# An mLSTM and window-attention layer: a convolution behind the first head's key scaling, and the first FFN weight casts behind the heads' last cast

## The chip, the cores and the metric

The kernel runs on one core of one Trainium2 chip. The time is the device time of one execution in microseconds. Before the change three runs took 1243.84, 1246.0 and 1246.75 us, median 1246.0. The execution that was profiled took 1243.28 us.

## The reference

One encoder layer on 1024 tokens of width 1024, in float32. One input projection feeds two groups of heads. Group A are four mLSTM heads of width 128, in both directions; group B are windowed attention heads. Their outputs are concatenated, projected, added to `alpha*x` and normalised; a gated feed-forward block with a second normalisation follows. The change touches group A and the way into the feed-forward block:

```python
qk = silu(centred_dwconv(x @ Wqk, conv_w, conv_b))      # 5 taps along the tokens, per channel
q, k = split(qk)                                         # 4 heads x 128 each
# per direction, per chunk of 64 tokens:
s   = einsum('td,sd->ts', qc, kc) * w_intra
num = s @ vc + w_inter * (C applied to qc)
h   = num / max(|den|, exp(-m))
C   = decay * C + einsum('s,se,sd->ed', wa, vc, kc)      # keys scaled by wa
# directions summed, normalised per head over its 128 channels, times norm_g * sigmoid(o)
x   = LN(alpha * x + concat(h, attention) @ Wout)
x   = LN(alpha * x + (silu(x @ Wg) * (x @ Wu)) @ Wo + sigmoid(x @ Wpg) * (p @ Wp))
```

## The kernel before

Every matmul is done as three (`mm3`, L126 to L129): each operand is split into a high and a low part (`split`, L106 to L113: ScalarE casts the high part, VectorE or GpSimd subtracts it for the low part), and high x high, high x low and low x high are summed in PSUM. TensorE (PE) is therefore the engine with the most work.

The stages follow each other: input projections and attention to about 226 us; the four mLSTM heads to about 434 us, with the remaining projections as fillers between a head's steps; the second half of the output projection and the first normalisation to about 500 us; the feed-forward block, the gate and its output projection to 1209 us; the second normalisation to the end.

What sets the order. The kernel is written with a scheduling framework: within a stage it decides, from its own cost table and due times, in which order each engine's instructions are put; an engine then runs its instructions strictly in that order. Two things bind the scheduler. While `strict[0]` is true (L333 to L551, and from L860 to L995), TensorE keeps the order of the program. And `tc.issue_after(ins)` puts what is issued inside it behind `ins` on the same engine; it is an order, not a semaphore. The heads' stage is left to the scheduler, so one new bound can move many instructions behind it.

A tile of the query and key projection is `qk_tile(ct)` (L287): tiles 0 and 1 are head 0's q and k, tile 2 is head 1's q, and so on. Each tile is made in two halves of 512 tokens in one of three PSUM banks `pj`; ScalarE copies a half into `pre` (L294; there is one buffer of that name), and VectorE then runs the convolution over 1024 tokens: one tensor_scalar (L297) and four scalar_tensor_tensor (L299). A Silu on ScalarE follows.

A head (`mlstm_head`, L571) does, for each half of its tokens: transposes of k into a PSUM bank `kp`; the key scaling `ks`, by ScalarE for the forward direction (L590) and by VectorE for the backward one (L593); later `pp` = q times k. `kp`, `pp` and `tr` (the transposes of the finished head) share two PSUM banks, so a `pp` can begin only when both scalings have read the `kp` that was in its bank. Then come the weights `mw` (a DMA, two GpSimd operations L624 and L631, exponentials on ScalarE, L628 on VectorE), the state updates `up` and `C`, four chunks of `nd`, their division and statistics, and one `rs` on GpSimd (L660), after which VectorE scales `hs` (L662) and TensorE transposes it.

At the end of the heads, `finish` (L678) splits the gated output `so` into `mh` (ScalarE) and `ml` (VectorE). `out_proj` (L688) multiplies it into `yo` and adds it to `y` (L699 for the half of the attention heads, L701 for the half of the mLSTM heads). Its banks are the three `pj` too. `wino_w1` (L837) loads the first weights of the feed-forward block, `rg`, and casts them: `a1h` on ScalarE, `a1l` on GpSimd.

Of the kernel before, what the change touches and what calls it, by code (L numbers as in the profile page):

```python
# [10 lines left out]
ALU = mybir.AluOpType  # L11
# [4 lines left out]
P = 128  # L16
D = 1024
S = 1024
# [17 lines left out]
def hybrid_layer(  # L36
# [7 lines left out]
    act, dve, pool = nc.scalar, nc.vector, nc.gpsimd  # L44
# [43 lines left out]
    def W(shape, dt, name, bufs=1, tag=None):  # L88
        return cur["wk"].tile(shape, dt, name=name, tag=tag or name, bufs=bufs)

    def X(shape, dt, name):
        return xp.tile(shape, dt, name=name, tag="X", bufs=NX)

    def Y(shape, dt, name):
        return yp.tile(shape, dt, name=name, tag="Y", bufs=8)

    def bank(name, tag):
        return cur["ps"].tile([P, 512], F32, name=name, tag=tag, bufs=cur["psn"][tag])

    def pjb(name):  # L100
        return pj.tile([P, 512], F32, name=name, tag="pj")

    def flat(t):
        return t.rearrange("p a b -> p (a b)")

    def split(dst_hi, dst_lo, src, eng_lo=None):  # L106
        act.copy(dst_hi, src)  # L107
        if eng_lo == "halves":
            for c in range(2):
                cs = slice(c * 512, c * 512 + 512)  # L110
                pool.tensor_tensor(dst_lo[:, cs], src[:, cs], dst_hi[:, cs].bitcast(F32), ALU.subtract)
            return
        (eng_lo or pool).tensor_tensor(dst_lo, src, dst_hi.bitcast(F32), ALU.subtract)  # L113

    def load_w(src, shape, name, eng_lo=None, raw=None):
# [4 lines left out]
        lo = wp.tile([P] + shape, F32R, name="lo_" + name, tag="wlo", bufs=4)  # L120
        split(flat(hi), flat(lo), flat(raw), eng_lo or "halves")
        return hi, lo

    last = {}

    def mm3(o, ah, al, bh, bl, start, stop, goes_on=False):  # L126
        pe.matmul(o, ah, bh, start=start, stop=False, skip_group_check=goes_on)
# [12 lines left out]
    def fill(n):  # L140
        while n:
            if not running:
                if not fillers:
                    return
                f = fillers.pop(0)
                f["load"]()
                for g in fillers[:1]:
                    g["load"]()
                running.append(f["body"]())
            with tc.high_priority(offset=-100):  # L150
                got = next(running[0], None)
            if got is None:
                running.pop()
            else:
                n -= 1
# [3 lines left out]
    def fillr():  # L159
        owed[0] += RM  # L160
        fill(int(owed[0]))
        owed[0] -= int(owed[0])

    def drain(n=0):
        while len(fillers) + len(running) > n:
            fill(1)
# [10 lines left out]
    def proj_T(src, name, evac):  # L177
        def body(w):
            wh, wl = w
            for hf in range(2):  # L180
                o = pjb("pj_" + name)
                for kt in range(KT):
                    kp, j = divmod(kt, 2)
                    mm3(o, wh[:, kt, :], wl[:, kt, :], xh[kp, hf][:, j, :], xl[kp, hf][:, j, :], kt == 0, kt == KT - 1)
                    yield 1
                evac(o, hf)
            done.add(name)

        return filler(lambda: load_w(src, [8, P], name), body)
# [69 lines left out]
    colt = const.tile([P, 8, 8], F32, name="colt")  # L259
# [27 lines left out]
    def qk_tile(ct):  # L287
        def evac(o, hf):
            if hf == 0:
                pre = qk["pre", ct] = prep.tile([P, S + 4], F32, name="pre", tag="pre")  # L290
                dve.memset(pre[:, 0:2], 0.0)
                dve.memset(pre[:, S + 2:S + 4], 0.0)
            pre = qk["pre", ct]
            act.copy(pre[:, 2 + hf * 512:514 + hf * 512], o)  # L294
            if hf == 1:
                y = qk[ct] = Y([P, S], F32, f"qk{ct}")
                dve.tensor_scalar(y, pre[:, 0:S], colt[:, ct, 0:1], colt[:, ct, 5:6], ALU.mult, ALU.add)  # L297
                for w in range(1, 5):
                    dve.scalar_tensor_tensor(y, pre[:, w:w + S], colt[:, ct, w:w + 1], y, ALU.mult, ALU.add)  # L299
                act.activation(y, y, AF.Silu)  # L300

        return proj_T(wqk[ct], f"qk{ct}", evac)
# [67 lines left out]
    cA, cWA, cFL, cDE = (gcol[:, i, :] for i in range(4))  # L370
# [186 lines left out]
    mh, ml = {}, {}  # L557
# [13 lines left out]
    def mlstm_head(h):  # L571
# [7 lines left out]
        ks = {}  # L579
        for hf in range(2):  # L580
            kp_ = bank("kp", "ma")
            for cc in range(4):
                c = hf * 4 + cc
                pe.transpose(kp_[:, cc * P:(cc + 1) * P], kT[:, c * P:(c + 1) * P], ident)
            for d in range(2):
                kk = W([P, 4, P], F32, f"ks{d}{hf}", 4, "ks")
                if d == 0:
                    for cc in range(4):
                        r = col(d, hf * 4 + cc)
                        act.activation(kk[:, cc, :], kp_[:, cc * P:(cc + 1) * P], AF.Copy, scale=cWA[:, r:r + 1])  # L590
                else:
                    r = col(d, hf * 4)
                    dve.tensor_tensor(kk, kp_.rearrange("p (c k) -> p c k", k=P),  # L593
                                      cWA[:, r:r + 4].unsqueeze(2).to_broadcast([P, 4, P]), ALU.mult)
                ks[d, hf] = kk
            fillr()
        orders = (list(range(8)), list(range(7, -1, -1)))
        for g in range(3):
            for d in range(2):
# [3 lines left out]
                for i, idx in enumerate(idxs):  # L603
                    c = order[idx]
                    last["up", g] = pe.matmul(up[:, i * 129:i * 129 + 129], ks[d, c // 4][:, c % 4, :], va_[:, c, :], start=True, stop=True)
                for i, idx in enumerate(idxs):
                    c, nx = order[idx], order[idx + 1]
# [6 lines left out]
        for hf in range(2):  # L614
# [5 lines left out]
            for d in range(2):  # L620
                mw = W([P, 4, 2, P], F32, f"mw{h}{hf}{d}", 4, "mw")
                nc.sync.dma_start(mw, mwd[d, h, hf * 4:hf * 4 + 4].rearrange("c q t -> (c q t)").unsqueeze(0).to_broadcast([P, 1024]))
                w = mw[:, :, 0, :]
                pool.tensor_tensor(w, mw[:, :, 0, :], maskb[:, d, :].unsqueeze(1).to_broadcast([P, 4, P]), ALU.add)  # L624
                for cc in range(4):
                    r = col(d, hf * 4 + cc)
# [10 lines left out]
            for cc in range(4):  # L637
                c = hf * 4 + cc
# [39 lines left out]
    def finish(h, hf):  # L678
        hp, hj = divmod(h, 2)
        if hj == 0:  # L680
            mh[hp, hf] = X([P, 2, 512], F32R, f"mh{hp}{hf}")
            ml[hp, hf] = X([P, 2, 512], F32R, f"ml{hp}{hf}")
        split(mh[hp, hf][:, hj, :], ml[hp, hf][:, hj, :], sod[h][:, hf * 512:hf * 512 + 512], dve)
# [4 lines left out]
    def out_proj(t, nh, kps, u, first):  # L688
        hf, tt = divmod(t, 4)
        s = slice(tt * P, (tt + 1) * P)  # L690
        o = pjb("yo")
        for kp in kps:
            for j in range(2):
                mm3(o, mh[kp, hf][:, j, s], ml[kp, hf][:, j, s], u[nh, kp][0][:, j, :], u[nh, kp][1][:, j, :],
                    kp == kps[0] and j == 0, kp == kps[1] and j == 1)
                yield 1
        ys = ya[t][:, nh * 512:nh * 512 + 512]
        if first:
            dve.scalar_tensor_tensor(ys, ys, ALPHA, o, ALU.mult, ALU.add)  # L699
        else:  # L700
            dve.tensor_tensor(ys, ys, o, ALU.add)  # L701
            if nh == 0:
                stat[t] = W([P, 2, 6], F32, "st1", 8)
            dve.bn_stats(stat[t][:, nh, :], ys)
# [20 lines left out]
    for h in range(MH):  # L725
        mlstm_head(h)
        if h:
            gated(h - 1, last["up", 0])
# [4 lines left out]
    gated(MH - 1, last["mm"])  # L733
    for hf in range(2):
        finish(MH - 1, hf)
    drain()

    scope_s.close()
# [61 lines left out]
    def ln1_tr(t, late=False):  # L800
        tt = t % 4
        if t == 0:
            bx["b11"], bx["b21"] = new_block((F4, F4), "b11"), new_block((F4, F4), "b21")
        if t == 4:
            bx["b22"] = new_block((F4, F4), "b22")
        if t < 4:
            tr_block((t, t + 1), 0, bx["b11"], tt, b_lo)
            tr_block((t, t + 1), 512, bx["b21"], tt, b_hi)
        else:
            tr_block((t, t + 1), 512, bx["b22"], tt, b_hi, late)  # L810
# [26 lines left out]
    def wino_w1(i, new):  # L837
        rg, ru = new(f"rg{i}"), new(f"ru{i}")
        nc.sync.dma_start(rg, wffi[i, 0])
        nc.sync.dma_start(ru, wffi[i, 1])  # L840
        if i < 2:
            p1 = [X([P, 8, P], F32R, f"a1{c}{i}") for c in "hl"]
        else:
            p1 = w_pair(i, 1)
        split(flat(p1[0]), flat(p1[1]), flat(rg), "halves" if i < 2 else dve)
        return rg, ru, p1

    def w_pair(i, k):
        return (wp.tile([P, 8, P], F32R, name=f"a{k}h{i}", tag="whi", bufs=4),
                wp.tile([P, 8, P], F32R, name=f"a{k}l{i}", tag="wlo", bufs=4))  # L850
# [10 lines left out]
    for t in range(NT):  # L861
        for nh in range(2):
            list(out_proj(t, nh, (0, 1), u, False))
            if (t, nh) in TR1:
                ln1_tr(TR1[t, nh])
            if (t, nh) == (7, 0):
                t_sums(0, (pool, dve))
            if (t, nh) == (3, 1):
                ws = [wino_w1(0, raw8), wino_w1(1, raw8f)]
        ln1_norm(t)  # L870


# [201 lines left out]
    for i in range(FT):  # L1074
# [6 lines left out]
        w = w2[i] if i < 2 else wino_w2(i, *ws[i])  # L1081
# [275 lines left out]
```

## Time and profile before

| | us |
|---|---|
| median of three runs | 1246.0 |
| the profiled execution | 1243.28 |
| its span in the trace | 1241.4 |
| TensorE busy within the span | 1206.1 |
| VectorE busy | 843.4 |
| ScalarE busy | 511.2 |
| GpSimd busy | 404.7 |

The span runs from the first to the last instruction in the trace; 1.9 us of the execution lie outside it. "Idle" of an engine is time without an instruction on it. A line such as `tr L60 <- DVE hs L662` says that TensorE's transposes at L60 waited for the tile `hs` that VectorE wrote at L662. PE is TensorE, DVE is VectorE, ACT is ScalarE, POOL is GpSimd and SP is SyncE, whose queue issues the DMAs.

### The profile page before, as it was taken

The page shows a single profiled execution, that of the slowest core. Times are in us where ns is not written, and L with a number is a line of the kernel's source. Part 1 is how long each engine was busy: PE and PEld are TensorE (multiplying, and loading weights), DVE is VectorE, ACT ScalarE, POOL GpSimd, SP SyncE. Part 2 cuts the span into 40 slices and gives each one's busy share as a digit, 9 for nine tenths or more (in the row PEclk, how much of TensorE's full clock was granted, in tenths as well). Part 3 has the DMA queues.
Part 4 walks back from the last instruction along what each step waited for, and adds up shares of the span by engine and source line. Part 5 has one row for each costly group of instructions (what it writes and reads, how often), then busy time and mean ns, then how long its engine had stood idle before and what let it go on. Part 6 is the DMA issues. An engine that isn't in the chain of part 4 may idle for free.

```text
span 1241.4 us, 16496 instructions
## 1 busy us (share of the span) xinstructions
PE 1206.1 (97%) x6017; PEld 1006.0 (81%) x6017; DVE 843.4 (68%) x1546; ACT 511.2 (41%) x920; POOL 404.7 (33%) x321
## 2 busy tenths in 40 slices
PE   8999999999989999899999999999999999999996
PEld 8888888788778877688888888888887888888885
DVE  6865545868778778856667577576568696555566
ACT  5655443544563234623334233343343333333331
POOL 4543322616334025612322223323227440000017
PEclk9999999999999999899999999999999999999998
DMA  6321112313174142134545453465335556666503
GB/s 232 102 88 69 44 60 93 116 34 120 51 261 151 59 140 85 35 128 130 217 165 193 165 206 135 162 218 188 128 118 209 208 187 219 192 197 189 186 1 135
DMA packets 68784, 174.39 MB, mean 140 GB/s; under 512 B 7328, under 2 KB 12128, under 8 KB 68704
## 3 DMA queue, kind: packets, MB, share of 16 engines
q1 hardware_dynamic: 68704, 173.35, 41.1%
q8 instruction: 47, 0.77, 0.3%
q14 instruction: 33, 0.27, 0.1%
HBM read 126.86 MB, written 46.47 MB: 140 GB/s over the span
## 4 chain that ended last, share of the span: by engine, by line
PE 79%; DVE 9%; DMA 3%; POOL 2%; issue 2%; ACT 2%; POOLq 0%; SPq 0%; ACTq 0%; DVEq 0%
PE ma L56 19%; PE mc L56 9%; PE oa L56 7%; PE ob L56 7%; PE yo L56 5%; PE pj_qk L56 5%; PE mb L56 4%; PE pg L56 4%; PE pn_v L56 3%; PE pj_aq L56 2%; PE pj_o L56 2%; PE op L56 2%; PE sp L56 1%; PE nd L56 1%; PE et L60 1%
## 5 line engine op out<-in xcount | busy, mean ns | idle before, releaser
L944 POOL TENSOR_TENSOR s<-ru,rg 128x512 f32<-128x512 f32 x22 | 30.0, 1364 | 179.7 <-DMA ru<-in_wffi_dram 163.3
L1273 POOL TENSOR_TENSOR rs<-rs,mhalf 128x1 f32<-128x1 f32 x8 | 9.4, 1184 | 183.0 <-DVE rs L1272 182.9
L499 POOL TENSOR_SCALAR e<-e,st 128x384 f32<-128x384 f32 (+1 forms) x64 | 35.0, 561 | 93.8 <-DVE st L497 54.7
L1015 DVE TENSOR_TENSOR us<-us,ma 128x512 f32<-128x512 f32 x22 | 15.1, 685 | 66.7 <-PE ma L56 66.7
L56 PE MATMUL yo<-hi_wo,mh 128*128 128x512 f32 x128 | 51.5, 403 | 2.6 <-DVE y L701 2.0
L299 DVE SCALAR_TENSOR_TENSOR qk<-pre,colt,qk 128x1024 f32<-128x1024 f32 x32 | 51.7, 1615 | 0.6
L56 PE MATMUL pj_qk<-xh,hi_qk 128*128 128x512 f32 x128 | 51.5, 402 | 0.0
L56 PE MATMUL pj_qk<-xl,hi_qk 128*128 128x512 f32 x128 | 50.7, 396 | 0.0
L56 PE MATMUL pj_qk<-xh,lo_qk 128*128 128x512 f32 x128 | 50.6, 396 | 0.0
L56 PE MATMUL yo<-lo_wo,mh 128*128 128x512 f32 x128 | 50.2, 392 | 0.0
L953 POOL TENSOR_TENSOR s<-ru 128x512 f32<-128x512 f32 x22 | 37.0, 1681 | 40.6 <-DVE a2l L113 36.9
L56 PE MATMUL yo<-hi_wo,ml 128*128 128x512 f32 x128 | 49.8, 392 | 0.0
L107 ACT CAST a2h<-s 128x512 fp32r<-128x512 f32 x44 | 25.9, 619 | 54.0 <-PE mc L56 39.5
L107 ACT CAST a4h<-s 128x512 fp32r<-128x512 f32 x22 | 13.7, 621 | 83.6 <-PE ma L56 49.1
L949 POOL TENSOR_TENSOR s<-rg,s 128x512 f32<-128x512 f32 x22 | 28.7, 1303 | 53.9 <-DVE a4l L113 53.9
L489 DVE CUSTOM_DVE_ANT_0 e<-sp,bias 128x384 f32<-128x384 f32 (+1 forms) x64 | 31.2, 521 | 19.7 <-PE sp L56 17.8
L495 ACT ACTIVATE e<-e,st 128x384 f32<-128x384 f32 (+1 forms) x64 | 37.2, 583 | 8.4 <-DVE st L491 8.4
L1010 DVE TENSOR_TENSOR yb<-yb,us 128x512 f32<-128x512 f32 x22 | 37.1, 1684 | 0.3 <-ACT yb L1009 0.3
L511 ACT COPY eT<-et 128x384 f32<-128x384 f32 (+1 forms) x32 | 14.4, 450 | 54.6 <-PE et L60 54.4
L921 DVE TENSOR_TENSOR sa<-sb,sa 128x512 f32<-128x512 f32 x11 | 8.1, 732 | 41.1 <-DMA sb<-in_wffo_dram 41.1
L56 PE MATMUL mb<-b21h,a1h 128*128 128x512 f32 x88 | 35.1, 399 | 0.7 <-DVE ya L1015 0.7
L624 POOL TENSOR_TENSOR mw<-mw,maskb 128x512 f32<-128x512 f32 x16 | 23.6, 1476 | 37.1 <-PE pj_o L56 17.7
(905 smaller groups left out, 4205.2 us busy)
## 6 DMA issues: line engine op xcount, KB each, us to landing
fb<-hb SPq DMA_DIRECT2D x35, 512.0 KB, 4.4
rg<-in_wffi_dram SPq DMA_DIRECT2D x22, 512.0 KB, 3.5
ru<-in_wffi_dram SPq DMA_DIRECT2D x22, 512.0 KB, 5.1
fa<-sb SPq DMA_DIRECT2D x20, 512.0 KB, 3.5
mw<-mwd SPq DMA_DIRECT2D x16, 512.0 KB, 5.3
fa<-in_wffo_dram SPq DMA_DIRECT2D x15, 512.0 KB, 3.8
hb<-ya SPq DMA_DIRECT2D x11, 512.0 KB, 3.8
hb<-yc SPq DMA_DIRECT2D x11, 512.0 KB, 2.9
```

Of the source, the lines that this page charges most:

```text
L56: return pe.put(nc.tensor.matmul(*args, **kw))
L107: act.copy(dst_hi, src)
L299: dve.scalar_tensor_tensor(y, pre[:, w:w + S], colt[:, ct, w:w + 1], y, ALU.mult, ALU.add)
L489: dve.tensor_tensor_reduce(e[:, i, :L], sp[:, :L], biasd[j][:, i, off:off + L], 1.0, -BIG, ALU.add, ALU.max, accum_out=st[:, i:i + 1])
L495: act.activation(e[:, i, :L], e[:, i, :L], AF.Exp, bias=st[:, i:i + 1], accum_out=st[:, 2 + i:3 + i])
L499: pool.tensor_scalar(e[:, i, :L], e[:, i, :L], st[:, 6 + i:7 + i], 0.0, ALU.mult, ALU.add)
L624: pool.tensor_tensor(w, mw[:, :, 0, :], maskb[:, d, :].unsqueeze(1).to_broadcast([P, 4, P]), ALU.add)
L944: pool.tensor_tensor(s3, ru[:, lo, :], rg[:, lo, :], ALU.subtract)
L949: pool.tensor_tensor(s4, rg[:, up, :], s2, ALU.subtract)
L953: pool.tensor_tensor(s1, ru[:, lo, :], ru[:, up, :], ALU.add)
L1010: dve.tensor_tensor(hb_, hb_, u, ALU.mult)
L1015: (eng or dve).tensor_tensor(dst, x, y_, ALU.add)
```

## The change

The convolution of tile 2 (head 1's q) is put behind `last["ks"]` on VectorE, the key scaling of head 0's second half. And the casts of the first two feed-forward weight tiles (`wino_w1(0)`, `wino_w1(1)`) are put behind `last["mh"]` on ScalarE, the last cast of the heads' output. Nothing is added to or taken out of the computation; one activation table load less is issued on ScalarE (857 instructions for 858). The counts of the other engines stay.

```diff
     def split(dst_hi, dst_lo, src, eng_lo=None):
-        act.copy(dst_hi, src)
+        last["hi"] = act.copy(dst_hi, src)
...
                 y = qk[ct] = Y([P, S], F32, f"qk{ct}")
-                dve.tensor_scalar(y, pre[:, 0:S], colt[:, ct, 0:1], colt[:, ct, 5:6], ALU.mult, ALU.add)
-                for w in range(1, 5):
-                    dve.scalar_tensor_tensor(y, pre[:, w:w + S], colt[:, ct, w:w + 1], y, ALU.mult, ALU.add)
+                with tc.issue_after(last["ks"].ins) if ct == 2 else ExitStack():
+                    dve.tensor_scalar(y, pre[:, 0:S], colt[:, ct, 0:1], colt[:, ct, 5:6], ALU.mult, ALU.add)
+                    for w in range(1, 5):
+                        dve.scalar_tensor_tensor(y, pre[:, w:w + S], colt[:, ct, w:w + 1], y, ALU.mult, ALU.add)
...
-                    dve.tensor_tensor(kk, kp_.rearrange("p (c k) -> p c k", k=P),
+                    last["ks"] = dve.tensor_tensor(kk, kp_.rearrange("p (c k) -> p c k", k=P),
...
         finish(MH - 1, hf)
+    last["mh"] = last["hi"]
...
             if (t, nh) == (3, 1):
-                ws = [wino_w1(0, raw8), wino_w1(1, raw8f)]
+                with tc.issue_after(last["mh"].ins):
+                    ws = [wino_w1(0, raw8), wino_w1(1, raw8f)]
```

The lines of the changed kernel are one to three higher than those of the kernel before. No engine's order changes ahead of about 232 us, and none changes from the first whole feed-forward block on (about 510 us). In between the scheduler's order changes on all of them.

VectorE at the end of head 0's key transposes; `qk_2483` is tile 2, `ks_2384` and `ks_2402` are head 0's two backward key scalings. Before:

```order
L297 TENSOR_SCALAR qk_2483<-pre,colt 128x1024
L299 SCALAR_TENSOR_TENSOR qk_2483<-pre,colt,qk_2483 128x1024 x2
L593 TENSOR_TENSOR ks_2384<-kp,gcol 128x512
L299 SCALAR_TENSOR_TENSOR qk_2483<-pre,colt,qk_2483 128x1024
L593 TENSOR_TENSOR ks_2402<-kp,gcol 128x512
```

and now:

```order
L594 TENSOR_TENSOR ks_2384<-kp,gcol 128x512
L594 TENSOR_TENSOR ks_2402<-kp,gcol 128x512
L298 TENSOR_SCALAR qk_2483<-pre,colt 128x1024
L300 SCALAR_TENSOR_TENSOR qk_2483<-pre,colt,qk_2483 128x1024
L610 COPY C_2372<-up 128x129
L300 SCALAR_TENSOR_TENSOR qk_2483<-pre,colt,qk_2483 128x1024
```

Both scalings now stand ahead of the convolution, and the first state copy and four `mw` operations have come between its pieces. TensorE waits for the scalings with `pp`; at the same place its rows read, before:

```order
L56 MATMUL up<-va,ks_2379 128x129 x3
L56 MATMUL pj_qk_2593<-xh_120,lo_qk_2361 128x512
L56 MATMUL pj_qk_2593<-xh_132,hi_qk_2360 128x512
L56 MATMUL pj_qk_2593<-xl_133,hi_qk_2360 128x512
L56 MATMUL pj_qk_2593<-xh_132,lo_qk_2361 128x512
L56 MATMUL pj_qk_2593<-xh_132,hi_qk_2360 128x512
L56 MATMUL pp<-qk_2225,qk_2344 128x128 x8
```

and now:

```order
L56 MATMUL up<-va,ks_2379 128x129 x3
L56 MATMUL pj_qk_2593<-xh_120,lo_qk_2361 128x512
L56 MATMUL pp<-qk_2225,qk_2344 128x128 x4
L56 MATMUL pj_qk_2593<-xh_132,hi_qk_2360 128x512
L56 MATMUL pj_qk_2593<-xl_133,hi_qk_2360 128x512
L56 MATMUL pp<-qk_2225,qk_2344 128x128 x4
```

The two `pp` of head 0 have come forward by four and two projection matmuls.

GpSimd at the second half of the third head (its weight tiles are `mw_3467` and `mw_3476`, forward and backward; the `rs` between belongs to the head before). Before:

```order
L624 TENSOR_TENSOR mw_3467<-mw_3467,maskb 128x4x128
L631 TENSOR_TENSOR mw_3467<-qk_2854,mw_3467 128x4x128
L660 TENSOR_TENSOR rs<-rs,mhalf 128x4
L624 TENSOR_TENSOR mw_3476<-mw_3476,maskb 128x4x128
L631 TENSOR_TENSOR mw_3476<-qk_2854,mw_3476 128x4x128
L113 TENSOR_TENSOR lo_wo_3765<-raw_wo_3762,hi_wo_3764 128x1024
```

and now:

```order
L625 TENSOR_TENSOR mw_3467<-mw_3467,maskb 128x4x128
L632 TENSOR_TENSOR mw_3467<-qk_2854,mw_3467 128x4x128
L625 TENSOR_TENSOR mw_3476<-mw_3476,maskb 128x4x128
L632 TENSOR_TENSOR mw_3476<-qk_2854,mw_3476 128x4x128
L661 TENSOR_TENSOR rs<-rs,mhalf 128x4
L115 TENSOR_TENSOR lo_wo_3771<-raw_wo_3768,hi_wo_3770 128x1024
```

The `rs` has moved behind two operations; a low part of an output weight still stands behind it, the next one of the four.

ScalarE at the end of the heads; `mh_4107` is the heads' last cast, `a1h_4558` the first feed-forward weight. Before:

```order
L653 ACTIVATE hs<-nd,den 128x128 x3
L107 CAST hi_wo_4343<-raw_wo_4341 128x1024
L107 CAST hi_wo_4349<-raw_wo_4347 128x1024
L107 CAST a1h_4558<-rg_4554 128x1024
L107 CAST mh_4107<-so_3844 128x512
```

and now:

```order
L654 ACTIVATE hs<-nd,den 128x128 x3
L109 CAST hi_wo_4343<-raw_wo_4341 128x1024
L109 CAST hi_wo_4349<-raw_wo_4347 128x1024
L109 CAST mh_4107<-so_3844 128x512
L109 CAST a1h_4558<-rg_4554 128x1024
```

The two casts have changed places.

## Rows read from the trace of the kernel before

**Rows 1.** The page, part 1: busy time, share of the span, instructions.

```profile
PE 1206.1 (97%) x6017; PEld 1006.0 (81%) x6017; DVE 843.4 (68%) x1546; ACT 511.2 (41%) x920; POOL 404.7 (33%) x321
```

**Rows 2.** The windows view: stretch, PE, PEld, DVE, ACT, POOL busy, PEclk, DMA share, GB/s.

```profile
527.00:930.00 403.00, 403.00 (x1780) 333.93 (x1779) 259.78 (x343) 143.08 (x231) 117.97 (x81) 1.00 0.47 165
```

**Rows 3.** Waits of PE, 205 to 600 us: us in total, times, longest.

```profile
PE tr L60 <- DVE hs L662: 3.9, 3, 1.8
...
PE pp L56 <- DVE ks L593: 2.2, 2, 1.2
PE yo L56 <- DVE y L701: 2.0, 2, 1.5
...
PE nd L56 <- DVE hs L654: 1.0, 1, 1.0
...
PE up L56 <- DVE C L611: 0.7, 1, 0.7
```

**Rows 4.** Timeline of PE: start us, us, instruction, [idle before <-releaser].

```profile
226.20 1.03 PE L60 MATMUL kp<-ident,qk 128*128 128x128 f32 x8
...
234.60 1.16 PE L56 MATMUL pp<-qk,qk 128*128 128x128 f32 x8 [1.21 <-DVE ks L593]
```

**Rows 5.** Timeline of DVE, same place.

```profile
228.37 1.11 DVE L297 TENSOR_SCALAR qk<-pre,colt 128x1024 f32<-128x1024 f32 x1 [5.48 <-ACT pre L294]
...
233.87 0.68 DVE L593 TENSOR_TENSOR ks<-kp,gcol 128x512 f32<-128x512 f32 x1
...
236.67 1.27 DVE L299 SCALAR_TENSOR_TENSOR qk<-pre,colt,qk 128x1024 f32<-128x1024 f32 x1
```

**Rows 6.** Timeline of ACT, same place.

```profile
231.59 1.12 ACT L590 ACTIVATE ks<-kp,gcol 128x128 f32<-128x128 f32 x4
...
238.94 0.56 ACT L294 COPY pre<-pj_qk 128x512 f32<-128x512 f32 x1
```

**Rows 7.** The windows view, behind the wait at 316 us; columns as Rows 2.

```profile
316.00:320.00 4.00, 3.62 (x11) 2.99 (x12) 4.00 (x8) 1.14 (x4) 0.24 (x1) 0.57 0.47 131
```

**Rows 8.** Timeline of PE, the wait at 360 us.

```profile
359.87 0.33 PE L60 MATMUL tr<-ident,hs 128*128 128x128 f32 x1 [1.53 <-DVE hs L662]
```

**Rows 9.** Timeline of DVE: three half heads' scalings of hs.

```profile
313.10 3.23 DVE L662 TENSOR_SCALAR hs<-hs,mv,rs 128x128 f32<-128x128 f32 x4 [1.14 <-POOL rs L660]
...
354.94 5.13 DVE L662 TENSOR_SCALAR hs<-hs,mv,rs 128x128 f32<-128x128 f32 x4 [0.16 <-POOL rs L660]
...
429.09 1.12 DVE L662 TENSOR_SCALAR hs<-hs,mv,rs 128x128 f32<-128x128 f32 x4
```

**Rows 10.** Timeline of POOL beside the second of them.

```profile
353.88 1.02 POOL L660 TENSOR_TENSOR rs<-rs,mhalf 128x4 f32<-128x4 f32 x1
...
356.12 1.29 POOL L631 TENSOR_TENSOR mw<-qk,mw 128x512 f32<-128x512 f32 x1
357.37 2.36 POOL L113 TENSOR_TENSOR lo_wo<-raw_wo,hi_wo 128x1024 fp32r<-128x1024 f32 x1
```

**Rows 11.** The chain that ended last, 436 to 442 us.

```profile
436.43 0.62 ACT mh L107
...
437.07 1.37 DVE ml L113
...
438.46 3.45 DMA y<-in_xn_dram
```

**Rows 12.** Timeline of all engines at the output projection's second half.

```profile
434.31 0.74 DVE L675 SCALAR_TENSOR_TENSOR so<-tr,colt,so 128x512 f32<-128x512 f32 x1
...
435.47 1.05 ACT L107 CAST a1h<-rg 128x1024 fp32r<-128x1024 f32 x1 [3.39 <-DMA rg<-in_wffi_dram]
...
438.36 0.67 DVE L701 TENSOR_TENSOR y<-y,yo 128x512 f32<-128x512 f32 x1
...
439.08 0.50 PE L56 MATMUL yo<-hi_wo,mh 128*128 128x512 f32 x1 [1.54 <-DVE y L701]
...
442.68 0.50 PE L56 MATMUL yo<-hi_wo,mh 128*128 128x512 f32 x1 [0.57 <-DVE y L699]
```

More of the change, by code (lines that the diff above doesn't have):

```diff
@@ L101, in pjb @@
         return pj.tile([P, 512], F32, name=name, tag="pj")
+    last = {}
     def flat(t):
@@ L122, in load_w @@
         return hi, lo
-    last = {}
     def mm3(o, ah, al, bh, bl, start, stop, goes_on=False):
@@ L592, in mlstm_head @@
                     r = col(d, hf * 4)
-                    dve.tensor_tensor(kk, kp_.rearrange("p (c k) -> p c k", k=P),
-                                      cWA[:, r:r + 4].unsqueeze(2).to_broadcast([P, 4, P]), ALU.mult)
+                    last["ks"] = dve.tensor_tensor(kk, kp_.rearrange("p (c k) -> p c k", k=P),
+                                                   cWA[:, r:r + 4].unsqueeze(2).to_broadcast([P, 4, P]), ALU.mult)
                 ks[d, hf] = kk
```

## The prediction

> **What bounds the kernel now.** The page's first part comes first: TensorE is busy for 1206.1 of 1241.4 us [rows 1], so only its idle time can be won, some 35 us. The windows view then says where none is: from 527 to 930 us TensorE is busy in all 403 of 403 us [rows 2]. What is won before that stage is thus not given back in it, and its order is not touched; a gain in the heads is a gain at the end. The list of TensorE's waits from 205 to 600 us names what there is to win around the change [rows 3]: transposes for the scaled head `hs` (3.9 us in three waits), the scores `pp` for the key scaling (2.2 in two), the output projection for `y` (2.0 in two), `nd` (1.0) and `up` (0.7). The two edits aim at the second and the third. The scheduler moves the places of the others too, so each gets a term.
>
> **The scores.** The keys are transposed at 226.20 in 1.03 us, and the first `pp` starts at 234.60 after 1.21 us of waiting [rows 4]. On VectorE the convolution of tile 2 begins at 228.37, after 5.48 idle us, and the first scaling runs only at 233.87 (0.68 us); the last piece ends at 236.67 + 1.27 = 237.94 [rows 5]. With the scalings ahead, both fit where VectorE was idle: from about 227.3 to 227.3 + 2 x 0.68 = 228.7, while ScalarE needs until 231.59 + 1.12 = 232.71 for its last one and about a scaling and an exponential less for the one before [rows 6]. ScalarE's scalings are now the later ones. By the order, three `up` and a projection matmul stand ahead of the first `pp`, so TensorE comes to it at about 232.5, and to the second at about 233.9, and both find their banks read. The whole 2.2 us go. The bounds are 0 (something in place of it) and 2.2.
>
> What is late next is the convolution: it starts some 0.3 us later, and the state copy and the `mw` operations are now in between. I put its end at 239.5 to 240.5, against 237.94. Behind it stand its Silu, for head 1's scores, which come after all of head 0's steps, and the one buffer `pre`: ScalarE's next copy into it, at 238.94 [rows 6], becomes about 2 us later. Of three PSUM banks one waits for that copy; one is being filled and one is free. A bank takes 24 matmuls; the twelve of an output projection's group take 442.68 - 0.57 - 439.08 = 3.03 us [rows 12], 0.25 each, so a bank takes 6 us. So 2 us are hidden; without that cover TensorE would lose them.
>
> **The first head's transposes.** The waits here are 3.9 less 1.53 [rows 8], or 2.4 us, and behind them TensorE runs at the lower clock: the granted clock is 0.57 from 316 to 320 us [rows 7], so x us of the four at half speed with 1 - 0.5x/4 = 0.57, x = 3.4, which costs 1.7 us. The chain is `nd`, division, statistics, `rs` on GpSimd, the scaling on VectorE. By the order 64 matmuls lie between that half head's last `nd` and its first transpose before the change, and 59 after; five at 0.25 us are 1.2 us of work. So TensorE gives the chain a little less time, and the chain's VectorE queue, which held the pieces of two convolutions, is a little emptier. I take 0.6 us gained, with the clock as it is; the bounds are 4.1 gained (wait and clock) and 1.2 lost.
>
> **The second head's `nd` and `up`.** Together 1.0 + 0.7 = 1.7 us. Both stand behind a scaling of `hs` that GpSimd's work slows, as below, and the order still has that scaling ahead of the state updates on VectorE. TensorE comes there earlier by what was won, and the scaling doesn't. I take 0.6 us lost; bounds 1.7 gained, 1.1 lost.
>
> **The transposes at 360 us.** The four scalings of a half head take 1.12 us where GpSimd is idle (429.09), 3.23 beside one `lo_wo` (313.10) and 5.13 beside an `mw` pair and a `lo_wo` (354.94) [rows 9]. The latter are GpSimd's rows: `rs` 353.88 to 354.90, a pair to 357.41, `lo_wo` to 359.73 [rows 10]; the wait of 1.53 us ends with the scaling [rows 8]. Now `rs` stands behind the pair, 2.5 us later. If `lo_wo` follows directly, the scaling takes 3.23 and ends 2.5 + 3.23 - 5.13 = 0.6 us later; if not, 1.12, and it ends 1.5 us earlier, which takes the wait away. I take 0.5 gained, the middle; bounds 1.5 gained, 0.6 lost.
>
> The Trainium skill, "SBUF — State Buffer" (Who interferes with whom), says that VectorE and GpSimd share one port pair and that the loser is fully blocked for a whole instruction of the other. The scalings agree in kind: four that take 1.12 us alone grew by 4.0 beside 4.9 us of GpSimd work. By that rule a `lo_wo` right behind `rs` would hold back one scaling for nearly all of its 2.36 us; this place would then be 0.6 lost, the total 1.1 us worse than mine; the slower rival (3) has the same mechanism at two places.
>
> **The output projection.** `so` is done at 434.31 + 0.74 = 435.05, but ScalarE waits 3.39 us for the weight `rg` and casts it at 435.47 for 1.05 us, ahead of `mh` [rows 12]; the chain has `mh` at 436.43 (0.62), `ml` at 437.07 (1.37), then the DMA of `y`, 3.45 us from 438.46 [rows 11], which waits for the buffer that `ml` frees. Now `mh` can run at 435.08, 1.35 us earlier, and `ml` beside an idle GpSimd: about 0.7 instead of 1.37, as half the work was waiting. `ml` ends at about 436.4 instead of 438.44. The wait of 1.54 us does not go as a whole: the matmuls of the group before end at 439.08 - 1.54 = 437.54, only one `pj` bank is free here (the attention half holds the two others until its `y` is there), and the addition to `y` takes 0.67 us [rows 12]. So the next group starts at about 438.3, 0.8 earlier. The DMA of `y` is issued 2.0 us earlier and lands at about 439.9, before the group ends at 441.3: the 0.57 us before 442.68 go too. Together 1.35 us; bounds 0 and 2.1 (both waits whole). The weight casts come about 0.3 us later, some 60 us ahead of the feed-forward block that uses them.
>
> **The sum.** -2.2 - 0.6 + 0.6 - 0.5 - 1.35 = -4.05 us, from 1243.28 to 1239.2. The median of the runs is 2.7 above the profiled execution, so 1242 us.
>
> **Rivals.** (1) The heads give the scores' gain back. For it: their chain begins with DMAs whose buffers come free when the half head before is done, and it has GpSimd and VectorE in it, neither of which gets faster; TensorE comes earlier to the same waits. Against: at most half heads no wait is listed, so the chain has slack there. Only the output projection's 1.35 us are left: about 1244.6.
> (2) The heads' waits go as well. For it: VectorE is the releaser in all of them, and the first wait is what the clock falls behind. 2.2 + 4.1 + 1.5 + 1.35 = 9.2 us gained, 1236.8. Against: `rs` and the slowed scalings remain.
> (3) Slower: scalings of `hs` blocked by GpSimd, with the `C` updates and `nd` divisions behind them in VectorE's queue. One costs 5.13 - 1.12 = 4.0 us of that queue; before, TensorE's share of it was 1.5 to 1.7 us. If the earlier TensorE meets two of them uncovered, 2 x (4.0 - 1.6) = 4.8 us are lost, and with one more stretch at the lower clock 1.7: 6.5 - 2.2 - 1.35 = 2.9 us slower, 1248.9. It decides the sign once the heads lose over 3.6 us. For it: three `rs` or `lo_wo` have changed places. Against: the pairs and `lo_wo` are no more than before.
> (4) That the change does not do what it says is excluded for the order, and the bank rule leaves no other reader for `pp`; it is part of (1).
>
> **Chances.** The forecast 0.50 (its own range 1240 to 1244), (1) 0.20, (2) 0.15, (3) 0.15. About 0.2%, 2.5 us, is what a measurement can tell here. Faster than that: 0.43 of the forecast, 0.03 of (1), all of (2), 0.61. Within it: 0.07 + 0.15, 0.22. Slower: 0.02 of (1), from the bounds, and (3), 0.17. The bounds summed reach from -11 to +3; 1236 to 1248 holds the forecast and (1), most of (2) and the near part of (3).
>
> **What would show it.** Right: no wait of `pp` for `ks`, the scalings on VectorE near 227.5, the convolution's end near 240 without a wait for a `pj` bank; `mh` ahead of `a1h`, the `yo` wait at some 0.7 us and that for L699 gone. Of the heads: the sum of TensorE's waits for `hs`, `C` and the divisions, now 5.6 us, and the stretch at the lower clock. If that sum grows by more than 3.6 us, the forecast is wrong and (3) is right; if it shrinks below 3, (2) is. If `pp` waits for ScalarE's scaling, the first term is.

## The result, and the profile after

| | before | after |
|---|---|---|
| median of four runs each | 1245.51 us | 1238.5 us |
| the profiled execution | 1243.28 us | 1237.98 us |
| its span | 1241.4 us | 1236.2 us |
| TensorE idle in the span | 35.3 us | 30.0 us |

The ratio is 0.994 with a 95% interval of 0.9926 to 0.9955: 5.6 to 9.2 us faster. A second series gave 1238.3 against 1246.15, ratio 0.9945 (0.993 to 0.996). The forecast was 1242, faster, with 1236 to 1248 as the range. The sign held and the size was too small. The difference of the profiled executions, which the terms of the sum are compared with, is 5.3 us. One execution in the experiments, the profiled one of `q_lodve`, took 2030.75 us at a mean granted clock of 0.557, and no number below uses it.

TensorE's busy time is the same (1206.2 us), so the gain is idle time. These are TensorE's waits from 205 to 600 us in the changed kernel; before, the first three lines of [rows 3] held 8.1 us:

```profile
PE x1s L60 <- DVE t3l L790: 3.3, 1, 3.3
PE yo L56 <- DVE y L700: 2.9, 3, 1.9
PE tr L60 <- DVE hs L663: 1.6, 1, 1.6
...
PE yo L56 <- DVE y L702: 1.2, 2, 0.8
...
PE ma L56 <- ACT a2h L109: 0.5, 1, 0.5
PE pj_qk L56 <- ACT pre L294: 0.3, 1, 0.3
PE pp L56 <- DVE ks L594: 0.2, 1, 0.2
```

The waits of `nd` and `up` [rows 3] and of the transposes at 360 us [rows 8] are gone as a whole, that of `pp` nearly. New are 0.3 us for `pre` and most of the 2.9 us for `y` at L700.

**The scores.** VectorE, then ScalarE, at the place of [rows 4 to 6]; the columns are start, duration, instruction, and in brackets the idle time and what ended it:

```profile
231.44 0.69 DVE L594 TENSOR_TENSOR ks<-kp,gcol 128x512 f32<-128x512 f32 x1 [9.19 <-ACT ks L591]
233.62 0.69 DVE L594 TENSOR_TENSOR ks<-kp,gcol 128x512 f32<-128x512 f32 x1 [1.49 <-ACT ks L591]
...
242.54 1.27 DVE L300 SCALAR_TENSOR_TENSOR qk<-pre,colt,qk 128x1024 f32<-128x1024 f32 x1
```

```profile
230.29 1.11 ACT L591 ACTIVATE ks<-kp,gcol 128x128 f32<-128x128 f32 x4
...
232.46 1.12 ACT L591 ACTIVATE ks<-kp,gcol 128x128 f32<-128x128 f32 x4
```

The scalings did not run near 227.5 but each right behind ScalarE's on the same bank: 230.29 + 1.11 = 231.40, then 231.44. VectorE stood idle for 9.19 us with the convolution queued behind, which ended at 243.81 and not near 240. On TensorE this left

```profile
234.37 1.16 PE L56 MATMUL pp<-qk,qk 128*128 128x128 f32 x8 [0.17 <-DVE ks L594]
...
245.43 0.50 PE L56 MATMUL pj_qk<-xh,hi_qk 128*128 128x512 f32 x1 [0.33 <-ACT pre L294]
```

so 2.25 us became 0.17, and the cover of the three `pj` banks was just used up, for 0.33 us.

**The heads.** Of the three scalings of `hs` that were slow before, the second and the `lo_wo` beside it are not among [rows 9] and [rows 10]; they read

```profile
337.48 5.17 DVE L662 TENSOR_SCALAR hs<-hs,mv,rs 128x128 f32<-128x128 f32 x4 [0.79 <-POOL rs L660]
...
339.93 2.39 POOL L113 TENSOR_TENSOR lo_wo<-raw_wo,hi_wo 128x1024 fp32r<-128x1024 f32 x1
```

The same three scalings now, and GpSimd's second, third and fourth `lo_wo`:

```profile
313.74 3.15 DVE L663 TENSOR_SCALAR hs<-hs,mv,rs 128x128 f32<-128x128 f32 x4
...
336.86 3.07 DVE L663 TENSOR_SCALAR hs<-hs,mv,rs 128x128 f32<-128x128 f32 x4
355.00 1.12 DVE L663 TENSOR_SCALAR hs<-hs,mv,rs 128x128 f32<-128x128 f32 x4 [0.15 <-POOL rs L661]
```

```profile
327.47 2.37 POOL L115 TENSOR_TENSOR lo_wo<-raw_wo,hi_wo 128x1024 fp32r<-128x1024 f32 x1 [11.17 <-ACT hi_wo L109]
...
344.43 2.37 POOL L115 TENSOR_TENSOR lo_wo<-raw_wo,hi_wo 128x1024 fp32r<-128x1024 f32 x1 [5.10 <-ACT hi_wo L109]
...
359.63 2.39 POOL L115 TENSOR_TENSOR lo_wo<-raw_wo,hi_wo 128x1024 fp32r<-128x1024 f32 x1 [4.66 <-ACT hi_wo L109]
```

The second and third scaling took 3.07 and 1.12 us, where before they took 5.17 and 5.13 (the latter in [rows 9]). The `lo_wo` that ran beside each of them before now runs earlier: the second of the four at 327.47 and no longer at 339.93, the third at 344.43 and no longer at 357.37. In GpSimd's order the second one now stands ahead of an `mw` pair and not behind it, and on ScalarE the casts `hi_wo` that the two wait for come earlier (326.26 and 343.31, before 333.29 and 353.89). So the `lo_wo` that comes next in GpSimd's order, behind the `mw` pair beside the second scaling and behind the `rs` ahead of the third, is the following one of the four. Its own cast is not done yet: GpSimd waits for it (5.10 and 4.66 us), and the third and fourth start 4.5 and 3.5 us behind the end of the scalings. GpSimd's order says that a `lo_wo` follows directly; the trace says that it follows with a wait.

**A new wait.** The chain that ended last, 391 to 402 us, and the windows behind it (stretch, busy times of PE, PEld, DVE, ACT, POOL, then PEclk, the granted clock):

```profile
391.23 1.26 POOL mw L632
...
392.50 3.60 DMA y<-in_xn_dram
...
396.13 0.70 DVE y L700
...
396.87 4.55 PE yo L56 x12
```

```profile
316.00:320.00 4.00, 3.56 (x18) 2.94 (x19) 3.93 (x6) 2.44 (x6) 0.29 (x1) 1.00 0.44 131
396.00:400.00 4.00, 3.13 (x10) 2.44 (x11) 3.34 (x5) 0.62 (x1) 0.00 (x0) 0.76 0.52 135
400.00:404.00 4.00, 3.54 (x14) 2.76 (x13) 2.13 (x12) 0.62 (x2) 0.00 (x0) 0.81 0.68 258
```

TensorE reaches the attention half's `yo` earlier than `y` is there: the DMA waits for the buffer of head 3's q, which GpSimd's last multiplication reads. 1.89 us at 396.87 and 0.46 at 402.18 are new. The clock's low stretch behind 316 us [rows 7] is gone; one behind 397 has come: (1 - 0.76) and (1 - 0.81) of 4 us at half speed, the lower of the clock's two levels, are 1.7 us lost, as before. That the stretch behind 316 us went is not shown to be the change's doing; `a_only` below still has it.

**The output projection.** The chain there, 431 to 438 us, and TensorE's starts:

```profile
431.39 0.63 ACT mh L109
...
432.05 0.70 DVE ml L115
...
432.77 4.61 DMA y<-in_xn_dram
```

```profile
430.85 0.47 PE L56 MATMUL yo<-hi_wo,mh 128*128 128x512 f32 x1 [0.44 <-DVE y L702]
434.61 0.50 PE L56 MATMUL yo<-hi_wo,mh 128*128 128x512 f32 x1 [0.78 <-DVE y L702]
438.14 0.50 PE L56 MATMUL yo<-hi_wo,mh 128*128 128x512 f32 x1 [0.51 <-DVE y L700]
```

`mh` starts 0.02 us after `so` and `ml` takes 0.70 for 1.37 us [rows 11], as worked out. Of the three waits the middle one fell by 0.76 us, and the last (0.57 before, [rows 12]) did not go, because this DMA took 4.61 us instead of 3.45. That is more than scatter. The load of `ru` for the feed-forward block is issued at 429.67 and lands at 434.39, so `y`, issued at 432.77, now runs beside it; before, `ru` had landed at 438.07 when `y` was issued at 438.46. The windows view of the two transfers, before and now, with the share of the DMA engines and GB/s last:

```profile
438.46:441.91 3.45, 2.83 (x12) 2.18 (x12) 1.63 (x4) 0.00 (x0) 1.65 (x2) 1.00 0.57 164
...
432.77:437.38 4.61, 3.83 (x17) 2.74 (x15) 1.74 (x4) 0.20 (x1) 3.08 (x3) 1.00 0.70 258
```

In the eight traces, here and in the experiments below, in which `y` is issued while `ru` is still landing, its DMA takes 4.16 to 5.95 us, in the three in which `ru` has landed (`before`, `a_only`, `b_lodve`) 3.40 to 3.58.

### The profile page after: what moved, and what is told of

Read it like the earlier page. It is cut to its first block, busy times and chain, and to the rows that moved or that the text cites. A ratio compares the mean times of both kernels' runs of the same rounds, so it can differ in the third digit from the quotient of the medians.

```text
span 1236.2 us, 16502 instructions
## 1 busy us (share of the span) xinstructions
PE 1206.2 (98%) x6017; PEld 1006.2 (81%) x6017; DVE 833.2 (67%) x1546; ACT 509.7 (41%) x919; POOL 397.2 (32%) x321
## 4 chain that ended last, share of the span: by engine, by line
PE 81%; DVE 6%; DMA 4%; POOL 2%; ACT 2%; issue 2%; SPq 0%; POOLq 0%; DVEq 0%; ACTq 0%
PE ma L56 19%; PE mc L56 9%; PE oa L56 7%; PE ob L56 7%; PE yo L56 6%; PE mb L56 5%; PE pj_qk L56 4%; PE pg L56 4%; PE pn_v L56 3%; PE pj_o L56 3%; PE pj_aq L56 2%; PE nd L56 2%; PE op L56 2%; PE sp L56 1%; PE et L60 1%
## 5 line engine op out<-in xcount | busy, mean ns | idle before, releaser
L300 DVE SCALAR_TENSOR_TENSOR qk<-pre,colt,qk 128x1024 f32<-128x1024 f32 x32 | 46.9, 1466 | 0.6
L56 PE MATMUL mb<-b21l,a1h 128*128 128x512 f32 x88 | 35.2, 400 | 0.0
```

Of the source, the lines that this page charges most:

```text
L56: return pe.put(nc.tensor.matmul(*args, **kw))
```

## The experiments

All ratios are to runs of the kernel before on the same chip.

**One part at a time.** `a_only` has the convolution's edit and leaves the weight casts as they were; `b_only` is the reverse.

```diff
-                with tc.issue_after(last["mh"].ins):
-                    ws = [wino_w1(0, raw8), wino_w1(1, raw8f)]
+                ws = [wino_w1(0, raw8), wino_w1(1, raw8f)]        # a_only
...
-                with tc.issue_after(last["ks"].ins) if ct == 2 else ExitStack():
+                with ExitStack():                                 # b_only
```

> Only the convolution of tile 2 is put behind the key scaling; the weight casts stay as before. Theory: this edit alone brings the scores' wait (2.25 us before, 0.17 after) and the heads' waits for hs, C and the division (5.55 before, 1.59 after), and pays the new waits for y near 397 and 402 us (2.35): against the kernel before a gain of 3.5 to 5.5 us, and the waits of the output projection's second half stay at 2.5 us. Rival: the heads' waits moved because of both edits; then the gain is the scores' 2 us alone, and waits for hs near 316, 344 and 360 us come back.

> Only the weight casts are put behind the heads' last cast. Theory: TensorE's order is that of before, so every wait of the heads is there (2.25 for the scores, 5.55 for the heads), and only the three waits between 430 and 443 us shrink, from 2.5 to about 1.7 us: a gain of 0.8 us, with an upper bound of 1.4, within the noise of 0.2%. Rival: the earlier DMA of y also takes the wait before the third group away, and the gain is 1.4 or more.

`a_only`: 1241.36 against 1245.88, ratio 0.9965 (0.9951 to 0.9978), 4.4 us faster. `b_only`: 1244.79, ratio 0.9989 (0.998 to 0.9998), 1.4 us faster. TensorE's waits in `a_only`, and in `b_only`:

```profile
PE yo L56 <- DVE y L700: 3.0, 3, 1.8
PE yo L56 <- DVE y L702: 2.1, 2, 1.7
PE tr L60 <- DVE hs L663: 1.6, 1, 1.6
...
PE pp L56 <- DVE ks L594: 0.2, 1, 0.2
```

```profile
PE tr L60 <- DVE hs L663: 4.5, 3, 1.9
...
PE pp L56 <- DVE ks L594: 2.5, 2, 1.4
...
PE yo L56 <- DVE y L702: 1.2, 2, 0.8
...
PE nd L56 <- DVE hs L655: 0.9, 1, 0.9
```

Up to 431 us `a_only` has the changed kernel's order on every engine, and `b_only` has TensorE's order of before throughout, so the waits gained and the new waits ahead of 430 us are the convolution's edit. The clock is another matter. In `a_only` the wait of 1.6 us at 316 us is followed by a low stretch,

```profile
316.00:320.00 4.00, 3.33 (x12) 2.67 (x13) 3.93 (x6) 1.95 (x5) 0.54 (x1) 0.67 0.41 131
320.00:324.00 4.00, 4.00 (x20) 3.30 (x19) 4.00 (x6) 2.52 (x4) 0.00 (x0) 0.91 0.00 0
```

1.7 us lost, where the changed kernel with the same order and the same wait had 1.00. The casts' edit shortens the waits for L702 alone, 2.0 to 1.2 us. Its interval holds 0.2 to 2.5 us, so its theory (0.8) and its rival (1.4) are not told apart.

**Without the slow neighbour.** `b_nolo` is the kernel before without GpSimd's four `lo_wo` of the attention half.

```diff
+        if eng_lo is pool:
+            act.copy(flat(hi), flat(raw))
+            return hi, hi
         lo = wp.tile([P] + shape, F32R, name="lo_" + name, tag="wlo", bufs=4)
```

> The kernel before, without the low parts of the attention half's output weights (GpSimd's four subtractions of 2.35 us are left out, and the high part is used in their place, so the output is not the reference's). TensorE's order through the heads up to about 400 us is that of before. Theory: the heads' waits come from scalings of hs that GpSimd's subtractions hold up; then the scaling at 313 falls from 3.23 to about 1.1 us, those at 337 and 355 from 5.1 to about 3, the waits of 2.35, 1.67 and 1.53 us shrink to under 2 in sum, and the half-clock stretch at 316 goes: 4 to 6 us less than before. Rival: the waits come from where TensorE's order puts the transposes and nd; then they stay and the gain is under 1 us.

1236.85, ratio 0.993 (0.9918 to 0.9943): 8.7 us faster, more than expected. Apart from the four `lo_wo`, every engine's order is that of before up to about 370 us, and yet TensorE's waits for `hs`, `C` and the division fall from 5.6 us to 0.5. The scalings at the same three places, and what is left of the wait:

```profile
315.25 1.11 DVE L665 TENSOR_SCALAR hs<-hs,mv,rs 128x128 f32<-128x128 f32 x4 [1.14 <-POOL rs L663]
335.60 3.08 DVE L665 TENSOR_SCALAR hs<-hs,mv,rs 128x128 f32<-128x128 f32 x4 [0.60 <-POOL rs L663]
351.10 3.07 DVE L665 TENSOR_SCALAR hs<-hs,mv,rs 128x128 f32<-128x128 f32 x4
```

```profile
PE tr L60 <- DVE hs L665: 0.5, 1, 0.5
```

So the heads' waits were made by `lo_wo` beside the scalings, not by where TensorE's order puts its steps. Where the gain beyond the expected 6 us comes from was not followed up.

**The same work on the other engine.** `b_lodve` is the kernel before, `a_lodve` the changed one, with `load_wout((2, 3), dve)` for `load_wout((2, 3), pool)`.

> The kernel before, with the four low parts of the attention half's output weights made by VectorE (1.23 us each) instead of GpSimd (2.35). Theory: what slows the scalings of hs is GpSimd at work beside them, not the amount of work; so most of the 9 us that leaving the subtractions out gave comes with the work kept: 4 to 8 us less than before. Rival: VectorE is as loaded as GpSimd is (23 to 24 of 31 us in the heads), the 4.9 us in its queue come back as waits for hs and C; less than 2 us gained or even slower.

> The changed kernel with the same low parts made by VectorE. Theory: only the wait of 1.59 us at 316 is left there for that cause, so 0 to 2 us less than the changed kernel, and the difference between the kernel before and the changed one shrinks when both have it, to 2 to 4 us. Rival: the two gains add up, 4 us or more less than the changed kernel.

`b_lodve`: 1239.88 against 1245.34, ratio 0.9953 (0.9936 to 0.9969). `a_lodve`: 1236.96, ratio 0.9933 (0.9916 to 0.995). In `b_lodve`, whose orders apart from `lo_wo` are those of before up to 315 us, the first scaling and the sum of TensorE's waits for `hs` read

```profile
314.56 1.11 DVE L662 TENSOR_SCALAR hs<-hs,mv,rs 128x128 f32<-128x128 f32 x4 [1.14 <-POOL rs L660]
```

```profile
PE tr L60 <- DVE hs L662: 2.7, 3, 1.1
```

and in `a_lodve` the scaling at 312.54 took 1.12. So what slows a scaling is GpSimd at work beside it, not the amount of work. The work is not free on VectorE, though: 2.7 us of waits for `hs` stay, and 5.5 us are gained where leaving the work out gave 8.7. With `lo_wo` on VectorE in both, 2.9 us are left between the two kernels, within the 2 to 4 expected. Against the changed kernel's own ratios, 0.994 and 0.9945, `a_lodve` is not told apart.

**The order of the two scalings.** `bwd_first0` is the changed kernel with VectorE's scaling issued ahead of ScalarE's in head 0.

```diff
-            for d in range(2):
+            for d in ((1, 0) if h == 0 else (0, 1)):
                 kk = W([P, 4, P], F32, f"ks{d}{hf}", 4, "ks")
```

> The changed kernel, with VectorE's scaling ahead of ScalarE's in head 0 alone. In the changed kernel VectorE was idle for 9.2 us until ScalarE's scalings ended and ran its own at 231.44 and 233.62, not at 227.5 as predicted. Theory: VectorE's scaling has to wait for ScalarE's read of the same PSUM bank; in the other order it runs near 227.5 and 228.2, the convolution of tile 2 ends 4 to 6 us earlier (243.8 in the changed kernel), and the 0.33 us in which TensorE waits for ScalarE's copy into pre goes, as does the 0.17 us of pp; 0 to 1 us less than the changed kernel. Rival: VectorE waits for the transposes or the factors, and its scalings start near 231 in this order too, with nothing gained.

1237.26 against 1245.34, ratio 0.9935 (0.9919 to 0.9951). VectorE:

```profile
228.60 1.29 DVE L594 TENSOR_TENSOR ks<-kp,gcol 128x512 f32<-128x512 f32 x2 [4.94 <-PE kp L60]
230.65 0.81 DVE L298 TENSOR_SCALAR qk<-pre,colt 128x1024 f32<-128x1024 f32 x1 [0.76 <-ACT pre L294]
231.50 7.96 DVE L300 SCALAR_TENSOR_TENSOR qk<-pre,colt,qk 128x1024 f32<-128x1024 f32 x4
```

Both scalings now follow the transposes, the convolution ends at 239.46, 4.35 us earlier, and neither `pp` nor `pj_qk` waits. The theory holds: ScalarE's read of the bank was what VectorE waited for. The 0.5 us that this gives are too few to tell in the total.

**Earlier `y`.** `qw_first` is the changed kernel with the last half head's multiplications ahead of its mask additions on GpSimd; `q_lodve` has the low parts on VectorE as well.

```diff
+            qfirst = (h, hf) == (MH - 1, 1)
+            if qfirst:
+                for mw in mws:
+                    lq = qw_mult(mw)
...
+                with tc.issue_after(lq.ins) if qfirst else ExitStack():
+                    pool.tensor_tensor(w, mw[:, :, 0, :], maskb[:, d, :].unsqueeze(1).to_broadcast([P, 4, P]), ALU.add)
```

> The changed kernel, and in the second half of the last head GpSimd's two multiplications by q come ahead of its two mask additions. Theory: the buffer that the DMA of y waits for at 392.50 us is head 3's q, which is free when the second multiplication ends; now that is at about 389.9, so y lands about 2.6 us earlier, the wait of 1.89 us before 396.87 goes and with it the stretch at the lower clock from about 398 to 401.6 (1.7 us) and most of the 0.46 at 402: against the changed kernel 3 to 4 us less, against before 8 to 10 less. Rival: the exponentials, which now come 2.6 us later, hold nd up instead, or y's DMA is held by the queue and not by the buffer: no gain, the waits stand elsewhere.

> As the last, with GpSimd's multiplications by q ahead of its mask additions in the last half head. Theory: the wait for y near 396 keeps its size of about 1.5 us less what DMA time varies, without the lower clock behind it; 1 to 3 us less than the changed kernel, the fastest version so far, near 1236. Rival: no gain over the run with the multiplications alone (1237.5).

`qw_first`: 1237.45, ratio 0.9941 (0.9929 to 0.9953), not told apart from the changed kernel's 0.994 and 0.9945, where 3 to 4 us less were expected. The chain there:

```profile
388.78 1.29 POOL mw L629
...
390.09 4.78 DMA y<-in_xn_dram
```

The buffer theory is right: the DMA is issued with the end of the second multiplication, 2.4 us earlier than at 392.50. But it took 4.78 us instead of 3.60, TensorE still waited 1.54 us, and 1.07 us at the next group, where VectorE's queue (the scalings, a `mw` operation and two low parts) stood ahead of the addition to `y`. Why it took 4.78 us is open; in `best`, which has this edit too, it took 3.64. `q_lodve`: 1235.83, ratio 0.9917 (0.9901 to 0.9934), as expected; it is judged by its times alone.

**All three, and the changed kernel again.** `best` has the three edits on the changed kernel.

> All three edits on the changed kernel: VectorE's scaling ahead of ScalarE's in head 0, the multiplications by q ahead of the mask additions in the last half head, and the attention half's low parts on VectorE. Theory: the three act at different places (230 to 245 us, 395 us, 316 us), so it is at or below the fastest so far, 1235.9, by the 0.5 us of the first place; 1234.5 to 1236.5. Rival: what comes earlier only waits longer for y near 396 us, and it is no faster than 1237.

> The changed kernel itself, unedited, beside the same runs of the kernel before. Theory: the edits add up, the convolution's 4.4 us and the casts' 1 to 1.5, so 5.5 to 6 us less than before. Rival: the 2.9 us between the changed kernel (1238.5) and the convolution's edit alone (1241.4) are real, the casts are worth more behind the other edit, and the difference stays at 7 us.

`best`: 1234.56 against 1246.15, ratio 0.9912 (0.9897 to 0.9927), 11 us faster than before and the lowest median of all, though its interval overlaps that of `q_lodve`. TensorE waits 0.87 us at L715 near 397, and the clock has no low stretch from 205 to 434 us. `after_again`: 1238.3. The medians differ by 7.9 us, and the parts add up to 5.8. The intervals (5.0 to 8.7 for the whole; 2.7 to 6.1 and 0.2 to 2.5 for the parts) overlap, so whether the casts are worth more behind the other edit stays open. Of the 3.8 us between the profiled executions of `a_only` (1241.82) and the changed kernel (1237.98), 1.7 are the low stretch at 316 us, which lies ahead of the casts and is not their doing.

## Why the prediction was right in sign and short in size

By its terms, in us of TensorE's waits:

| term | forecast | measured |
|---|---|---|
| scores | -2.2 | -2.1, and +0.3 for `pre` |
| first head's transposes | -0.6, clock as it is | -0.8, and no low stretch in this execution (-1.7) |
| second head's `nd` and `up` | +0.6 | -1.7 |
| transposes at 360 us | -0.5 | -1.5 |
| output projection | -1.35 | -0.8 |
| `yo` near 397 and 402 us | none | +2.35, and a low stretch (+1.7) |
| entry of the feed-forward block | none | -1.6 |

The first step that failed is the one on the second head: "Both stand behind a scaling of `hs` that GpSimd's work slows". In the changed kernel it was slowed by one pair instead of a pair and a `lo_wo`, 3.07 us for 5.17, and the wait went. The same holds for the transposes at 360 us: I took the middle between `lo_wo` following directly and not, and it did not. These two terms were 0.1 us lost in the sum and 3.2 gained on the chip; that is more than the whole difference between 4.05 and 5.3. I had read GpSimd's order and not asked which of the four `lo_wo` stands there and when its operand `hi_wo` is ready. That `lo_wo` is the cause of the waits before is shown by `b_nolo`, and of the slow scaling by `b_lodve`, not only by where it stands. The Trainium skill, "SBUF — State Buffer" (Who interferes with whom), says that of VectorE and GpSimd on their shared port pair the loser is blocked for a whole instruction of the other. The trace agrees: the worst single scaling before took 2.45 us, where the median is 0.34 and a `lo_wo` takes 2.36. But at 360 us no `lo_wo` stood beside the scaling any more, so the loss of 0.6 us worked out by that rule did not come.

The scores' size was right for a wrong reason. "Both fit where VectorE was idle" was false: on each bank VectorE follows ScalarE. I listed both as readers of the bank and overlooked that they don't read it together. The Trainium skill, "PSUM — Partial Sum Buffer" (PSUM bank collisions raise a hardware error), says that two engines must not access one bank at once, reads included, and that semaphores have to keep them apart; the trace agrees, with 0.04 us between the end of one and the start of the other. The convolution therefore ended at 243.81 and not near 240, and TensorE waited 0.33 us for a bank, against the signs that the prediction gave. What saved the term is that TensorE reaches the second `pp` so late that 0.17 us were left.

The new wait for `y` is what rival (1) names, TensorE coming earlier to a chain that does not get faster, at a place where no wait was listed before. I had looked for it at the places with a wait only. In the output projection the first wait shrank as worked out (0.78 for the 0.7 forecast); the step that failed is the DMA of `y`, taken at its 3.45 us although it now starts beside the load of `ru`. Rival (3) did not come: no scaling got slower where TensorE waited for it (one did, 4.53 us at 374.01, with no wait behind it). Of rival (2) the half on `nd`, `up` and the transposes at 360 us came. By the sign that the prediction gave, a sum of the waits for `hs`, `C` and the divisions below 3 us, it is rival (2) that holds: the sum fell from 5.6 to 1.6. The measured 1238.5 also lies outside the forecast's own range of 1240 to 1244 and nearer to that rival's 1236.8. The price of rival (2) leaves out the 1.7 us of `nd` and `up`; with them it is 10.9 us and not 9.2, and the bounds summed reach to -11.6 and not -11.

That the total came within 1.8 us of the sum is in part luck: against the forecast, by the table, 5.1 us more were gained (second head, 360 us, first head, entry of the feed-forward block), and 3.3 us more were lost (`yo`, the output projection, the scores).

The measured column adds up to -5.85 us, the two changes of the clock cancelling in these two executions; TensorE's idle time fell by 5.3. What the entry of the feed-forward block gained (the wait of 1.28 us for `b22l` before 507.90, and 0.27 of `ma`) was not followed up; in the experiments that wait is between nothing and 1.4 us. The span fell by 5.2 us in one execution each, the medians by 7.0 and 7.9; the difference is smaller than the scatter of executions, below.

## What to carry to other kernels

Ask of every instruction that a reordering moves not only what stands ahead of it on its engine but when its operands are there: an order list shows neighbours that the trace does not. Where two engines read one PSUM bank, issue first the reader whose engine is free first; an engine that is put ahead of other work to read a bank can stand idle for the other reader. A transfer that is issued earlier can meet another one in flight and take longer. And if a chain-bound stage gets faster, look for the next wait at the places where the slack was, not only where waits are listed.

## What the runs showed of the hardware

The low stretch of TensorE's clock is not tied to a place or to the length of one wait. With two waits for `pp` of 1.21 and 1.04 us the granted clock stayed at 1.00 in the kernel before, and with 1.44 and 1.05 us, at the same place, it was 0.79 from 234 to 242 us in `b_only`; a wait of 1.61 us at 316 was followed by one in `a_only`, one of 1.59 us in the changed kernel was not; a wait of 1.89 us near 397 was followed by a low stretch in the changed kernel, one of 1.86 us in `bwd_first0` was not. Each of these stretches costs about 1.7 us, as much as the wait before it. Executions of one kernel here lie up to 6.3 us apart (the kernel before, 1243.84 to 1250.11 in one series). Part of that goes with this clock: over the 39 executions of the kernel before in the experiments, the mean granted clock lies between 0.989 and 0.994, and the time falls by some 0.7 us for each 0.001 of it, with a correlation of -0.48, so by this estimate about a quarter of the variance.

Near the output projection's second half the transfer of `y` took 3.40 to 3.58 us behind the landing of `ru` and 4.16 to 5.95 us beside it, and four scalings of `hs` took 1.1 us beside an idle GpSimd and 5.1 us beside its three operations.
